# Token chunks of 512 and 784 instead of 656 and 640 in a two-pass hybrid encoder layer

## The chip, the core and the metric

The kernel runs on one core of a Trainium2 chip. The metric is the device time of one execution in microseconds (us); lower is better. Engines are named as the profile names them: PE (TensorE), PEld (its weight loads), DVE (VectorE), ACT (ScalarE), POOL (GpSimd) and SP (SyncE, which issues all DMAs here).

## What is computed

One encoder layer is applied to two requests: 1024 prompt tokens and 256 sample tokens, each preceded by the same 16 meta tokens; the width is 2048. The reference, cut down:

```python
u = rms_norm(h, norm_w) @ w_in                     # 2048 -> 6656 = 52 strips of 128
qa, ka, va, za, qb, kb, vb, zb = split(u)          # 8, 2, 2, 8, 8, 8, 8, 8 strips
qa, ka = rope(rms_norm(qa)), rope(rms_norm(ka));  qb, kb = rms_norm(qb), rms_norm(kb)
ya = global_gqa(qa, ka, va) * silu(za)             # 8 heads, 2 KV groups, all tokens
yb = neighbourhood_attention(qb, kb, vb, rpb) * silu(zb)   # 8 heads, window 8 x 16 + meta
return h + concat(ya, yb) @ w_out
```

## The kernel before

**Precision.** Every fp32 operand is split into a high part (rounded to fp32r) and a low part (the rest), and each product is three matmuls: high x high, high x low, low x high (`strips`, lines 131 to 133). Splitting a tile is a cast on ACT (line 50) and a subtraction on DVE (line 51).

**Two chunks.** All 16 + 256 + 1024 tokens don't fit on chip with the working buffers, so the input projection goes over the weights twice. Chunk 1 has the 16 meta tokens, the 256 sample tokens and the first 384 prompt tokens (T1 = 656); chunk 2 has the other 640 prompt tokens (T2). In a chunk the normalised x stays resident as 16 tiles (`kt`) of 128 rows, high and low. For each of the 52 strips, `strips` goes through 16 `kt`, and for each `kt` through the token blocks of the chunk. A block is one PSUM tile of at most 512 columns, so a chunk has two blocks: 272 + 384 (k and v strips) or 256 + 384 (q and z strips) in chunk 1, and 384 + 256 in chunk 2. That is 52 x 16 x 4 x 3 = 9984 matmuls.

**Weights.** In chunk 1 a strip's weights come in four DMAs (line 114), are split (lines 50 and 51), and the low part is also stored to DRAM (line 124). In chunk 2 the low part is read back (line 118) and only the cast on ACT is done again (line 119).

**x tiles.** `get_x` (lines 73 to 103) loads one `kt` into a ring of four tiles named `xr` (line 77; one of the four is held by the running sum `xacc`), ACT makes the high part (line 81), DVE the low part (82), ACT squares the ring tile in place (86) and DVE adds it to `xacc` (87), after which the ring tile is free. It is called from `strips` at the moment the first strip of a chunk needs that `kt`. The rings, the attention work buffers and all other pools are opened once in `build` (from line 957) and live through both chunks.

**Attention.** Chunk 1 runs the sample's 16 heads as their strips are done; the last two strips (v and z of the last head) are projected together, and then that head's attention runs. Its work tiles are `Sm`, `zs` (pool `mx`) and the six `t` tiles; the last of them is read by `put_y` (lines 229 to 239). In the second half of chunk 1 sums of `w_out` blocks are also made (`w_sums`: per projection either four loads or four stores of 256 KB). Chunk 2 first projects k and v of the first KV group together, then runs the prompt's 8 global heads (three strips and four query blocks for each), and then 24 remaining strips of the local heads between 28 blocks of local attention. v is turned into rows by PE transposes (line 173). `outproj` follows with its own pools; its matmuls (lines 827 to 829) have 320 columns.

The instructions are put in order by a scheduler at build time; every engine and the SP queue then run their lists in that order.

Of the kernel before, what the change touches and what calls it, by code (L numbers as in the profile page):

```python
# [27 lines left out]
C1P = 384  # L28
# [12 lines left out]
QA, KA, VA, ZA, QB_, KB, VB, ZB = 0, 8, 10, 12, 20, 28, 36, 44  # L41


class Kern:
# [27 lines left out]
    def get_x(self, kt):  # L72
        nc = self.nc
        if kt not in self.xs:
# [3 lines left out]
            h = self.x.tile([P, T], F32R, tag="xh", name="xh")  # L78
            l = self.x.tile([P, T], F32R, tag="xl", name="xl")
            w = self.nw[:, kt:kt + 1]  # L80
            nc.scalar.activation(h[:], r[:], AF.Copy, scale=w)  # L81
            nc.vector.scalar_tensor_tensor(out=l[:], in0=r[:], scalar=w, in1=h[:].bitcast(F32), op0=ALU.mult, op1=ALU.subtract)  # L82
# [5 lines left out]
            self.xs[kt] = (h[:], l[:])  # L88
            if kt == KT - 1:
                with self.tc.issue_after(self.lastx):  # L90
                    for d, c in self.consts:
                        nc.sync.dma_start(d[:], c)
# [4 lines left out]
                for o in range(0, T, 328):  # L97
                    n = min(328, T - o)
                    rr = self.rsqrt(self.eb[:, o:o + n], n)
                    nc.scalar.mul(self.rb[:, o:o + n], rr[:], -1.0)  # L100
# [3 lines left out]
    def strips(self, jobs, getx):  # L104
# [297 lines left out]

    def copy_km(self, k):
# [11 lines left out]
    def meta_tiles(self):  # L415

        self.npm = 0
        self.pms = [self.sm.tile([P, QB], F32R, tag=f"Pm{i}", bufs=1, name="Pm") for i in range(2)]
        self.vm3 = self.v.tile([P, P], F32R, tag="vm", name="vm3")
# [39 lines left out]
    def chunk1(self):  # L459
# [3 lines left out]
        ct = self.tab.tile([P, T1], F32, tag="bt", name="ropec")  # L463
        st = self.tab.tile([P, T1], F32, tag="st", name="ropes")
        B0, B1, BQ = (0, NMETA + NS), (NMETA + NS, C1P), (NMETA, NS)

        def k_strip(s, g, wc, rope):
            kt_ = self.k.tile([P, 2, T1], F32R, tag="k1", name="kc1")

            def evac(ps):  # L470
                for p, (o, n) in zip(ps, [B0, B1]):
                    rp = (ct[:, o:o + n], st[:, o:o + n]) if rope else None
                    self.qk_evac(p, o, n, wc, rp, [(0, n, kt_[:, 0, o:o + n], kt_[:, 1, o:o + n])])
                nc.sync.dma_start(self.kd[g][:, :, :NMETA], kt_[:, :, :NMETA].bitcast(F32))
                nc.sync.dma_start(self.kd[g][:, :, NMETA:], kt_[:, :, NMETA + NS:].bitcast(F32))
                return kt_, self.copy_km(kt_)
            return s, [B0, B1], evac

        def v_strip(s, g):
# [3 lines left out]
            vp = self.v.tile([P, 3 if loc else 6, P], F32 if loc else F32R, tag="v1", name="vp")  # L483

            def evac(ps):
                vt = self.v_rows(ps[0], *B0)
                tp = self.v_turn(vt, [0], NMETA)
                self.split(vm[:, 0:1, :], vm[:, 1:2, :], tp)
# [4 lines left out]
                vt = self.v_rows(ps[1], *B1)  # L493
                tp = self.v_turn(vt, [0, P, 2 * P])
                if loc:
                    nc.scalar.copy(vp[:], tp)
                    nc.sync.dma_start(self.vn[g - 2][:C1P].rearrange("(t p) d -> p t d", p=P), vp[:])
                else:
                    self.split(vp[:, :3, :], vp[:, 3:, :], tp)
                    nc.sync.dma_start(self.vd[g][:], vp[:].bitcast(F32))  # L500
# [3 lines left out]
            return s, [B0, B1], evac  # L504

        def q_strip(s, h, wc, rope):
            q = self.s.tile([P, 2, QB], F32R, tag="S", name="qs")

            def evac(ps):
                qp = [self.ev.tile([P, C1P], F32R, tag="ev", name="qp") for _ in range(2)]  # L510
                for p, (o, n), d in zip(ps, [BQ, B1], [(q[:, 0, :], q[:, 1, :]), (qp[0][:], qp[1][:])]):
                    rp = (ct[:, o:o + n], st[:, o:o + n]) if rope else None
                    self.qk_evac(p, o, n, wc, rp, [(0, n, *d)])
# [3 lines left out]
            return s, [BQ, B1], evac  # L517

        def z_strip(s, h):
            z = self.mx.tile([P, QB], F32, tag="mx", name="zs")  # L520

            def evac(ps):
                zp = self.ev.tile([P, C1P], F32, tag="ev", name="zp")
                self.z_evac(ps[0], *BQ, [(0, NS, z[:])])
                self.z_evac(ps[1], *B1, [(0, C1P, zp[:])])
                nc.sync.dma_start(self.zd[h][:, :C1P], zp[:])
                return z
            return s, [BQ, B1], evac
# [38 lines left out]
    def chunk2(self):  # L567
# [3 lines left out]
        ct = self.tab.tile([P, T2], F32, tag="bt", name="ropec2")  # L571
        st = self.tab.tile([P, T2], F32, tag="st", name="ropes2")
        self.consts = [(ct, io["ropec"][:, T1:]), (st, io["ropes"][:, T1:])]
        BL = [(0, 384), (384, 256)]
# [18 lines left out]
        def v_strip(s, g):  # L593

            v = [self.v.tile([P, 8, P], F32R, tag=f"v{i}", name="va") for i in range(2)]
            vm = self.load_vm(g)
            for i in range(2):
                nc.sync.dma_start(v[i][:, :3, :].bitcast(F32), self.vd[g][:, 3 * i:3 * i + 3, :])

            def evac(ps):  # L600
                for p, (o, n) in zip(ps, BL):
                    j, e = 3 + o // P, 3 + (o + n) // P
                    self.split(v[0][:, j:e, :], v[1][:, j:e, :], self.v_turn(self.v_rows(p, o, n), range(0, n, P)))
                return [(v[0][:, j, :], v[1][:, j, :]) for j in range(8)], vm
            return s, BL, evac

        def v_local(s, h):

            def evac(ps):
                for p, (o, n) in zip(ps, BL):  # L610
                    j, e = 3 + o // P, 3 + (o + n) // P
                    vt = self.ev.tile([P, n // P, P], F32, tag="ev", name="vl")
                    nc.scalar.copy(vt[:], self.v_turn(self.v_rows(p, o, n), range(0, n, P)))
                    nc.sync.dma_start(self.vn[h][P * j:P * e].rearrange("(t p) d -> p t d", p=P), vt[:])
            return s, BL, evac

        def v_windows(h):

            v = []
            for i in range(2):  # L620
                t = self.v.tile([P, 8, P], F32, tag=f"v{i}", name="vw")
                for j in range(2):
                    o = 32 * WIN0[2 * i + j]
                    nc.sync.dma_start(t[:, 4 * j:4 * j + 4, :], self.vn[h][:].rearrange("(t p) d -> p t d", t=4)[o:o + P])
# [92 lines left out]
        for h in range(NH):  # L717
            late += [qk_late(KB + h, kwb, self.k2d[2 + h]), qk_late(QB_ + h, qwb, self.q2d[8 + h]),
                     z_late(ZB + h, self.zd[8 + h]), v_local(VB + h, h)]
# [5 lines left out]
        for g in range(2):  # L725
            if g == 0:
                k, v = pr(k_strip(KA, 0, kw, True), v_strip(VA, 0))
            else:
                k, = pr(k_strip(KA + g, g, kw, True))
                v, = pr(v_strip(VA + g, g))  # L730
# [28 lines left out]
    def y_load(self, p, k):  # L759
# [6 lines left out]
        return [half(*x) for x in {1: [(k, 0)], 2: [(8 + k, 0)], 4: [(8 + k, 1)], 7: [(k, 0), (k, 1)],  # L766
                                   5: [(k, 1), (8 + k, 1)], 6: [(k, 0)], 3: [(8 + k, 0)]}[p]]

    def y_operand(self, p, k, r):
        nc = self.nc  # L770
        if p in (1, 2, 4):
            v = r[0]
        elif p == 7:
# [98 lines left out]
    def outproj(self, end_attention):  # L872
# [22 lines left out]
        for n in range(N):  # L895
# [19 lines left out]
            if n > 6:  # L915
# [14 lines left out]
    def build(self):  # L930
# [3 lines left out]
        with tc.tile_pool(name="dr", bufs=1, space=DRAM) as dp, tc.tile_pool(name="const", bufs=1) as cp, \  # L934
                tc.tile_pool(name="raw", bufs=4) as self.raw, tc.tile_pool(name="w", bufs=4) as self.w:
            self.kd = [dp.tile([P, 2, NMETA + C1P], F32, name=f"kd{g}") for g in range(10)]
            self.vd = [dp.tile([P, 6, P], F32, name=f"vd{g}") for g in range(2)]
            self.vn = [dp.tile([NP, P], F32, name=f"vn{h}") for h in range(NH)]
# [14 lines left out]
            with ExitStack() as ps, ExitStack() as es_y:  # L953
# [5 lines left out]
                es_pp, es_x, es_attn, es_xr, es_proj, es_late = (ExitStack() for _ in range(6))  # L959
                pool(es_pp, "pp", 4, space=PSUM)  # L960
                pool(es_x, "x", 16, side="right")
# [99 lines left out]
```

## Time and profile before

| | |
|---|---|
| median of 3 runs | 2250.45 us (2248.92 to 2253.45) |
| the profiled execution, its own time | 2249.38 us |
| its span, first to last instruction | 2247.6 us |
| PE busy | 2218.2 us, 99% of the span |
| DVE, ACT, POOL busy | 71%, 51%, 23% |

Matmuls overlap in the profile (each row reaches over the start of the next), so the time that one takes on PE is read from start to start, and not from the mean duration of a group. A granted clock of 1.00 is 2.4 GHz.

### The profile page before, as it was taken

To read this page: it belongs to the slowest core of one execution; us is meant where nothing else is said; L and a number is where in the kernel's file an instruction comes from. 1 tells how busy PE (TensorE), PEld (TensorE's weight loads), DVE (VectorE), ACT (ScalarE), POOL (GpSimd) and SP (SyncE) were. 2 spreads that over 40 slices of the span, in tenths; PEclk is the share of its full clock that TensorE was granted. 3 is DMA by queue.
4 is the path that set the end of the run, shared out by engine and by line. 5 is a ranking of instruction groups with operands and counts; after the bars stand their busy time and mean duration, and the time that the engine had idled before them with its cause. 6 is when DMAs were issued, how large, how long until landed. Compare 5 with 4: busy or idle time off the path is not lost.

```text
span 2247.6 us, 42246 instructions
## 1 busy us (share of the span) xinstructions
PE 2218.2 (99%) x15550; PEld 2208.7 (98%) x15550; DVE 1596.4 (71%) x2988; ACT 1141.5 (51%) x2432; POOL 526.5 (23%) x275
## 2 busy tenths in 40 slices
PE   7999999999999999999999999999999999999999
PEld 6999999999999999999999999999999999999999
DVE  5876677656666566999979998887665677636743
ACT  5554554443444466777667776655444454232220
POOL 0322222222222203332323332343333222000000
PEclk9999999999999999999999999999999999999999
DMA  7656578777777775444454344476767664845663
GB/s 238 196 185 185 176 225 254 246 238 246 243 243 235 228 241 152 126 122 123 140 149 126 112 134 138 151 219 207 221 201 215 211 194 127 276 152 162 198 210 112
DMA packets 279856, 424.54 MB, mean 189 GB/s; under 512 B 48576, under 2 KB 121184, under 8 KB 279648
## 3 DMA queue, kind: packets, MB, share of 16 engines
q1 hardware_dynamic: 279648, 421.84, 61.1%
q8 instruction: 122, 2.00, 0.4%
q14 instruction: 86, 0.70, 0.1%
HBM read 296.25 MB, written 118.90 MB: 185 GB/s over the span
## 4 chain that ended last, share of the span: by engine, by line
PE 90%; DVE 4%; DMA 3%; ACT 1%; POOL 1%; issue 1%; SPq 0%; DVEq 0%; POOLq 0%; ACTq 0%
PE pp L132 20%; PE pp L133 20%; PE pp L131 20%; PE pq L827 6%; PE pq L829 6%; PE pq L828 6%; DMA xr<-in_x 2%; PE po L392 1%; PE po L295 1%; PE po L293 1%; PE po L294 1%; PE sp L253 1%; PE sp L254 1%; PE sp L255 1%; DVE S L273 1%
## 5 line engine op out<-in xcount | busy, mean ns | idle before, releaser
L131 PE MATMUL pp<-xh,wh 128*128 128x384 f32 (+2 forms) x3328 | 1026.9, 312 | 16.9 <-ACT xh L81 16.9
L133 PE MATMUL pp<-xh,wl 128*128 128x384 f32 (+2 forms) x3328 | 1035.2, 312 | 0.0
L132 PE MATMUL pp<-xl,wh 128*128 128x384 f32 (+2 forms) x3328 | 1034.1, 311 | 0.4 <-DVE xl L82 0.2
L131 PEld LDWEIGHTS pp<-xh,wh 128*128 128x128 f32 x3328 | 625.7, 189 | 19.5 <-ACT xh L81 19.2
L132 PEld LDWEIGHTS pp<-xl,wh 128*128 128x128 f32 x3328 | 628.0, 189 | 1.8 <-DVE xl L82 1.8
L133 PEld LDWEIGHTS pp<-xh,wl 128*128 128x128 f32 x3328 | 628.1, 189 | 0.7
L51 DVE TENSOR_TENSOR wl<-wr,wh 128x512 fp32r<-128x512 f32 x320 | 236.4, 751 | 177.5 <-ACT wh L50 164.2
L141 POOL PARTITION_ALL_REDUCE m<-ms x104 | 237.0, 2279 | 399.6 <-ACT ms L139 264.0
L50 ACT CAST wh<-wr 128x512 fp32r<-128x512 f32 x320 | 193.7, 618 | 225.2 <-PE pp L132 150.9
L827 PE MATMUL pq<-ym,wh 128*128 128x320 f32 x896 | 276.5, 309 | 1.3 <-DVE vt L166 1.3
L828 PE MATMUL pq<-ym,wh 128*128 128x320 f32 x896 | 277.0, 309 | 0.0
L829 PE MATMUL pq<-ym,wl 128*128 128x320 f32 x896 | 276.9, 309 | 0.0
L222 POOL PARTITION_ALL_REDUCE tot<-a x80 | 168.4, 2105 | 439.7 <-DVE a L220 432.8
L205 POOL PARTITION_ALL_REDUCE ma<-m x80 | 114.2, 1427 | 460.3 <-DVE m L203 460.1
L827 PEld LDWEIGHTS pq<-ym,wh 128*128 128x128 f32 x896 | 168.2, 188 | 1.5 <-ACT ym L50 1.5
L829 PEld LDWEIGHTS pq<-ym,wl 128*128 128x128 f32 x896 | 168.3, 188 | 0.0
L828 PEld LDWEIGHTS pq<-ym,wh 128*128 128x128 f32 x896 | 168.3, 188 | 0.0
L119 ACT CAST wh<-wr 128x512 fp32r<-128x512 f32 x208 | 127.8, 615 | 56.5 <-PE pp L132 54.9
L57 ACT ACTIVATE rs_l<-m 128x384 f32<-128x384 f32 (+2 forms) x104 | 49.1, 472 | 121.4 <-DVE m L142 119.1
L257 ACT COPY S<-sp 128x512 f32<-128x512 f32 x136 | 78.6, 581 | 51.6 <-PE sp L255 45.0
L51 DVE TENSOR_TENSOR pl<-S,ph 128x512 fp32r<-128x512 f32 x136 | 98.7, 733 | 7.5 <-ACT ph L50 7.1
L61 DVE TENSOR_TENSOR rs_l<-m,rs_l 128x384 f32<-128x384 f32 (+2 forms) x104 | 75.4, 725 | 33.6 <-ACT rs_l L60 33.5
(200 smaller groups left out, 3396.9 us busy)
## 6 DMA issues: line engine op xcount, KB each, us to landing
wr<-in_w_in SPq DMA_DIRECT2D x416, 256.0 KB, 3.8
wld<-wl SPq DMA_DIRECT2D x208, 256.0 KB, 4.3
wl<-wld SPq DMA_DIRECT2D x208, 256.0 KB, 3.3
yr<-yd SPq DMA_DIRECT2D x72, 320.0 KB, 4.2
wq<-in_w_out SPq DMA_DIRECT2D x64, 256.0 KB, 5.5
td<-wq SPq DMA_DIRECT2D x64, 256.0 KB, 4.6
wr<-td SPq DMA_DIRECT2D x64, 256.0 KB, 3.6
wr<-in_w_out SPq DMA_DIRECT2D x48, 256.0 KB, 4.2
```

The costliest lines, as they stand in the source:

```text
L50: nc.scalar.copy(hi, full)
L51: return nc.vector.tensor_tensor(out=lo, in0=full, in1=hi.bitcast(F32), op=ALU.subtract).ins
L119: nc.scalar.copy(wh[:], w[:])
L131: nc.tensor.matmul(p[:, :n], wh[:, k, :], xh[:, o:o + n], start=first, stop=False)
L132: nc.tensor.matmul(p[:, :n], wh[:, k, :], xl[:, o:o + n], start=False, stop=False)
L133: nc.tensor.matmul(p[:, :n], wl[:, k, :], xh[:, o:o + n], start=False, stop=last)
L141: nc.gpsimd.partition_all_reduce(m2[:], ms[:], P, RED.add)
L205: nc.gpsimd.partition_all_reduce(ma[:], m1[:], P, RED.max)
L222: nc.gpsimd.partition_all_reduce(tot[:], a1[:], P, RED.add)
L827: nc.tensor.matmul(ps[:, b, :B], wh, yh[:, o], start=k == 0, stop=False)
L828: nc.tensor.matmul(ps[:, b, :B], wh, yl[:, o], start=False, stop=False)
L829: nc.tensor.matmul(ps[:, b, :B], wl, yh[:, o], start=False, stop=k == 7)
```

## The change

The first chunk gets 240 prompt tokens (T1 = 512), the second 784. Chunk 1 then has one block of 512 columns (k, v) or 496 (q, z), and chunk 2 two blocks of 392, for each product. 16 strips (q, k, v and z of local heads 4 to 7) neither store nor reload their low weight parts: chunk 2 splits them again. Chunk 1's pools are closed at its end, and chunk 2 opens its own in the same memory; a tile of a pool opened with `reuse_waits: "tile"` waits only for the old tiles that it lies over. Chunk 2 makes all of its 16 x tiles before its first strip, and the `xr` ring is then closed and the attention work pools are opened in its place. The v rows of all strips go through DRAM. Ring depths: `raw` 5 in chunk 1 and 3 afterwards (4 before), `ev` 8 in chunk 2 (9), `y` 1 in chunk 2 (2). In the output projection some operands are loaded straight into their final tile and split there.

```diff
-C1P = 384
+C1P = 240
+AGAIN = {a + h for a in (QB_, KB, VB, ZB) for h in range(4, 8)}
...
-                    if self.second:
+                    if self.second and s not in AGAIN:
...
-                if not self.second:
+                if not self.second and s not in AGAIN:
...
+    def rows_out(self, vt, n, dst, o):
...
+                nc.tensor.transpose(tp[:m, i, :], vt[:, x:x + m], self.ident[:])
...
+            nc.scalar.copy(t[:, :f, :], tp[:, :f, :])
+            nc.sync.dma_start(dst[o + a:o + a + P * f].rearrange("(t p) d -> p t d", p=P), t[:, :f, :])
...
-        B0, B1, BQ = (0, NMETA + NS), (NMETA + NS, C1P), (NMETA, NS)
+        B0, BQ = (0, T1), (NMETA, NS + C1P)
...
+        for kt in range(KT):
+            self.get_x(kt)
+        open_attention()
+        BL = [(0, T2 // 2), (T2 // 2, T2 // 2)]
...
+        def v_tiles(g):
...
+            nc.sync.dma_start(l[:].bitcast(F32), self.vn[g][:].rearrange("(t p) d -> p t d", p=P))
...
+        if p in (1, 2, 4):
+            t = self.ym.tile([P, 2, TH], F32R, tag="ym", name="ym")
+            self.nc.sync.dma_start(t[:, 1, :].bitcast(F32), self.yd[k if p == 1 else 8 + k][:, TH * (p == 4):][:, :TH])
+            return t
...
+                work = (("s", 5), ("ph", 2), ("sm", 2), ("mx", 2), ("t", 6))
...
+                with ExitStack() as es_1:
+                    pool(es_1, "x", 16, side="right")
+                    for name, bufs in (("raw", 5), ("tab", 1), ("k", 1), ("v", 1), *work, ("y", 2), ("one", 1), ("ev", 9), ("xr", 4)):
+                        pool(es_1, name, bufs)
+                    self.chunk1()
...
+                pool(es_x, "x", 16, side="right", **kw)
+                for name, bufs in (("one", 1), ("ev", 8)):
+                    pool(es_proj, name, bufs, side="right", **kw)
+                for name in ("k", "v", "tab", "q", "z"):
+                    pool(es_attn, name, 1, **kw)
+                pool(es_xr, "xr", 4, **kw)
...
+                def open_attention():
+                    es_xr.close()
+                    for name, bufs in (*work, ("y", 1)):
+                        pool(es_attn, name, bufs, **kw)
```

## Rows read from the trace of the kernel before

**Rows 1.** The page, busy time of each engine over the span.
```profile
PE 2218.2 (99%) x15550; PEld 2208.7 (98%) x15550; DVE 1596.4 (71%) x2988; ACT 1141.5 (51%) x2432; POOL 526.5 (23%) x275
```
**Rows 2.** The page, shares of the chain that ended last, by engine.
```profile
PE 90%; DVE 4%; DMA 3%; ACT 1%; POOL 1%; issue 1%; SPq 0%; DVEq 0%; POOLq 0%; ACTq 0%
```
**Rows 3.** Windows: stretch, length, busy us (instructions) per engine, PEclk, DMA share, GB/s.
```profile
0.00:50.00 50.00, 35.40 (x186) 32.20 (x187) 30.46 (x39) 29.36 (x42) 1.31 (x9) 0.97 0.73 222
...
805.00:840.00 35.00, 31.43 (x208) 30.56 (x208) 26.44 (x45) 26.29 (x49) 3.87 (x2) 0.95 0.80 257
1450.00:1900.00 450.00, 445.52 (x3182) 443.69 (x3182) 319.18 (x709) 228.99 (x519) 146.51 (x86) 1.00 0.65 200
...
1950.00:2000.00 50.00, 50.00 (x343) 50.00 (x342) 25.18 (x36) 16.49 (x29) 0.00 (x0) 1.00 0.62 200
```
**Rows 4.** PE groups by shape: count, busy us, mean ns of one, idle before.
```profile
L133 PE MATMUL pp<-xh,wl 128*128 128x384 f32 x1664 | 564.6, 339 | 0.0
...
L133 PE MATMUL pp<-xh,wl 128*128 128x256 f32 x1344 | 379.2, 282 | 0.0
...
L829 PE MATMUL pq<-ym,wl 128*128 128x320 f32 x896 | 276.9, 309 | 0.0
```
**Rows 5.** PE timeline around 1101 us: start, duration, instruction.
```profile
1100.67 0.34 PE L131 MATMUL pp<-xh,wh 128*128 128x384 f32 x1
...
1101.20 0.28 PE L131 MATMUL pp<-xh,wh 128*128 128x256 f32 x1
...
1102.27 0.34 PE L131 MATMUL pp<-xh,wh 128*128 128x384 f32 x1
...
1102.79 0.28 PE L131 MATMUL pp<-xh,wh 128*128 128x256 f32 x1
```
**Rows 6.** Waits of PE, whole span: total us, times, longest.
```profile
PE pp L131 <- ACT xh L81: 16.9, 8, 7.9
```
**Rows 7.** ACT timeline, the first and the last x tile of chunk 1.
```profile
7.01 0.84 ACT L81 ACTIVATE xh<-xr,nw 128x656 fp32r<-128x656 f32 x1 [0.26 <-DMA xr<-in_x]
...
46.77 0.84 ACT L81 ACTIVATE xh<-xr,nw 128x656 fp32r<-128x656 f32 x1 [0.60 <-DMA xr<-in_x]
```
**Rows 8.** SP timeline, two x loads of chunk 2, seven others between them.
```profile
807.19 0.33 SPq L77 DMA_DIRECT2D xr<-in_x  x1
...
831.76 0.33 SPq L77 DMA_DIRECT2D xr<-in_x  x1
```
**Rows 9.** Line 82: durations ns min/median/max; then the landing of line 77's DMAs.
```profile
L82 DVE SCALAR_TENSOR_TENSOR xl<-xr,nw,xh x32: 865/890/904, 7.9 to 838.5; 128x656 fp32r<-128x656 f32 x16, 128x640 fp32r<-128x640 f32 x16
...
DMA to landing us min/median/max: 2.8/4.5/6.7
```
**Rows 10.** PE timeline, first matmul after chunk 1's last strips.
```profile
804.99 0.19 PE L307 MATMUL sp<-qs,kc 128*128 128x64 f32 x1
```
**Rows 11.** DVE timeline, the last head of chunk 1: last readers of Sm and of tot.
```profile
823.13 1.21 DVE L215 TENSOR_TENSOR Pm<-Sm,Pm 16x256 fp32r<-16x256 f32 x1
...
830.58 0.41 DVE L232 SCALAR_TENSOR_TENSOR r<-tot,r 128x256 f32<-128x256 f32 x1
```
**Rows 12.** The chain, output matmuls of two sample heads in turn.
```profile
396.42 0.84 PE po L332 x8
457.00 0.84 PE po L332 x8
```
**Rows 13.** Windows of chunk 1, columns as in rows 3.
```profile
365.00:370.00 5.00, 5.00 (x37) 5.00 (x36) 4.20 (x8) 1.46 (x3) 0.00 (x0) 1.00 1.00 353
...
665.00:670.00 5.00, 5.00 (x36) 5.00 (x35) 2.69 (x6) 2.71 (x6) 0.00 (x0) 1.00 0.99 297
...
300.00:550.00 250.00, 250.00 (x1719) 249.65 (x1718) 169.18 (x305) 110.57 (x242) 58.44 (x28) 1.00 0.79 244
```
**Rows 14.** Groups by shape: the transposes, the low parts of the weights.
```profile
L173 PE MATMUL tp<-ident,vt 128*128 128x128 f32 x116 | 19.2, 272 | 0.0
...
L51 DVE TENSOR_TENSOR wl<-wr,wh 128x512 fp32r<-128x512 f32 x320 | 236.4, 751 | 177.5 <-ACT wh L50 164.2 <-DMA wr<-in_w_in 6.3 <-DMA wld<-wl 3.4
```

More of the change, by code (lines that the diff above doesn't have):

```diff
@@ L96, in get_x @@
                 nc.vector.tensor_scalar(out=self.eb[:], in0=self.eb[:], scalar1=EPS, scalar2=None, op0=ALU.add)
-                for o in range(0, T, 328):
-                    n = min(328, T - o)
+                for o in range(0, T, 392):
+                    n = min(392, T - o)
                     rr = self.rsqrt(self.eb[:, o:o + n], n)
@@ L401, in bias_table @@
         return tab
+    def rows_out(self, vt, n, dst, o):
+        nc = self.nc
+        for a in range(0, n, 4 * P):
+            offs = range(a, min(n, a + 4 * P), P)
+            full = [x for x in offs if x + P <= n]
+            t = self.ev.tile([P, 3, P], F32, tag="ev", name="vl")
+            tp = self.tp.tile([P, 4, P], F32, tag="tp", name="tp")
+            for i, x in enumerate(offs):
+                m = min(P, n - x)
+                nc.tensor.transpose(tp[:m, i, :], vt[:, x:x + m], self.ident[:])
+            f = len(full)
+            nc.scalar.copy(t[:, :f, :], tp[:, :f, :])
+            nc.sync.dma_start(dst[o + a:o + a + P * f].rearrange("(t p) d -> p t d", p=P), t[:, :f, :])
+            if f < len(offs):
+                m = n - offs[f]
+                t = self.ev.tile([m, P], F32, tag="ev", name="vl")
+                nc.scalar.copy(t[:], tp[:m, f, :])
+                nc.sync.dma_start(dst[o + n - m:o + n], t[:])
     def copy_km(self, k):
@@ L417, in meta_tiles @@
         self.npm = 0
-        self.pms = [self.sm.tile([P, QB], F32R, tag=f"Pm{i}", bufs=1, name="Pm") for i in range(2)]
-        self.vm3 = self.v.tile([P, P], F32R, tag="vm", name="vm3")
+        self.pms = [self.mt.tile([P, QB], F32R, tag=f"Pm{i}", name="Pm") for i in range(2)]
+        self.vm3 = self.mt.tile([P, P], F32R, tag="vm", name="vm3")
         for t in (*self.pms, self.vm3):
@@ L482, in v_strip @@
             vm = self.v.tile([NMETA, 2, P], F32R, tag="vm1", name="vm")
-            vp = self.v.tile([P, 3 if loc else 6, P], F32 if loc else F32R, tag="v1", name="vp")
             def evac(ps):
                 vt = self.v_rows(ps[0], *B0)
-                tp = self.v_turn(vt, [0], NMETA)
-                self.split(vm[:, 0:1, :], vm[:, 1:2, :], tp)
+                self.split(vm[:, 0:1, :], vm[:, 1:2, :], self.v_turn(vt, [0], NMETA))
                 if loc:
@@ L492, in evac @@
                     self.split(vs[:, :2, :], vs[:, 2:, :], self.v_turn(vt, [NMETA, NMETA + P]))
[L493 to L500, printed above, removed]
+                self.rows_out(vt[:, PS:], C1P, self.vn[g], 0)
                 for i, j in enumerate((0, 1, 0)):
@@ L516, in evac @@
                 return q
[L517 removed]
+            return s, [BQ], evac
         def z_strip(s, h):
@@ L771, in y_operand @@
         if p in (1, 2, 4):
-            v = r[0]
-        elif p == 7:
+            self.split(r[:, 0, :], r[:, 1, :], r[:, 1, :].bitcast(F32))
+            return r
+        if p == 7:
             v = r[0]
@@ L934, in build @@
         with tc.tile_pool(name="dr", bufs=1, space=DRAM) as dp, tc.tile_pool(name="const", bufs=1) as cp, \
[L935 removed]
+                tc.tile_pool(name="raw", bufs=3) as self.raw, tc.tile_pool(name="w", bufs=4) as self.w:
             self.kd = [dp.tile([P, 2, NMETA + C1P], F32, name=f"kd{g}") for g in range(10)]
[L937 to L938 removed]
+            self.vn = [dp.tile([NP, P], F32, name=f"vn{g}") for g in range(10)]
             self.vmd = [dp.tile([M3, P], F32, name=f"vmd{g}") for g in range(10)]
```

99 lines of the change are left out of this document (40 added, 59 removed).

## The prediction

> **What bounds the kernel now.** I read the page first: PE is busy 99% of the span and the next engine, DVE, 71% [rows 1], and the chain that ended last is 90% PE [rows 2]. So only two things can move the time: what PE's own work costs, and the few places where PE waits. The windows show where these are [rows 3]: 14.6 us without PE in the first 50 us, 3.6 us between 805 and 840 us, 4.5 us in all of 1450 to 1900 us. The list of PE's waits names the cause of the largest: 16.9 us for the high part of an x tile [rows 6]. At 805 to 840 us the granted clock is 0.95 of 2.4 GHz as well, so 5% of 35 us is 1.8 us of lost PE work there, 5.3 us in all.
>
> **Term 1, matmuls.** The columns stay the same (1296 for k and v, 1280 for q and z); the blocks per product go from four to three, so 52 x 16 x 3 = 2496 of 9984 matmuls go. What one of them costs beyond its columns is read in two ways. Start to start, six 384-column matmuls take 0.53 + 0.52 us and nine 256-column ones 1.07 us [rows 5]: 175.0 and 118.9 ns, a slope of 0.438 ns per column, which leaves 6.7 ns at no columns. The 320-column ones take 50 us / 343 = 145.8 ns [rows 3]; with the slope of the mean durations, (339 - 282) / 128 = 0.445 [rows 4], 3.3 ns is left. I take the middle, 5 ns: 2496 x 5 = **-12 us**. Bounds: with the slope of the upper pair, (339 - 309) / 64 = 0.469, the fixed part is 145.8 - 150 = below zero, so 0; with one column per cycle at 2.4 GHz it is 145.8 - 133.3 = 12.5 ns, so -31 us. My value lies near the lower end because both long baselines do.
>
> The Trainium skill ("TensorE: Matmul & The Clock Gate", section "Wait — 56ns, not 53.3ns?") gives a warm matmul N / 2.4 GHz plus about 2.5 ns whatever N is. This trace does not agree: 320 columns take 12.5 ns more than N / 2.4. By the page's fixed part the term would be an estimated 2496 x 2.5 ns = -6 us, and the sum below 6 us higher.
>
> **Term 2, the way from chunk 1 to chunk 2.** Before, the x ring outlives chunk 1, so x tiles of chunk 2 are loaded while the last strips run. After, the ring lies where chunk 1's work tiles were. From the pool list: chunk 1 puts raw (10,240 bytes per partition), tab (4608), k (4480), v (3072), s (10,240), ph (8192), sm (2048), mx (4096) and t (6144) one after another; chunk 2 puts k (8704), v (8192), tab (6272), q (8192) and z (4096), so its ring begins at 35,456 and has four tiles of 3136. The first two lie over ph and the first Sm, both long free; the third over the second Sm and mx, the fourth over the last head's `zs` and a `t` tile. Of the four, one is `xacc`. With two early places, at least one of the first three users (first x tile, `xacc`, second x tile) gets a late one; I assume both of the latter do. So the first x tile can come early, and the next, and the sum that frees the first, wait for the last head's attention.
>
> Let E be the end of chunk 1's last strips (804.99 us in this trace [rows 10]). That head's Sm was last read from 823.13 us on, its tot at 830.58 [rows 11]: 18 and 26 us after E, shared with the x tiles' own ACT and DVE work. With those held back I estimate 10 and 14 us; bounds 5 and 26. A ring tile's round is load, high part, low part, square, sum, each after the other. In the first chunk 16 tiles of 656 columns went from 7.01 to 46.77 us [rows 7], 2.65 us each; times 784/656 is 3.2. In the second, nine loads from 807.19 to 831.76 us [rows 8] are 3.07 us apart at 640 columns, beside attention; times 784/640 is 3.8. I take 3.1: of the round only the transfer and the four passes grow, the landing (2.8 to 6.7 us [rows 9]) has a part that does not. The fourth tile's load then starts at E + 15, lands and is cast by E + 20, and the last of the 16 is ready at 20 + 12 x 3.1 = E + 57; its matmuls end at E + 59. PE's own work up to there is 16 x 12 matmuls of 392 columns (0.179 us: 5 ns and 0.445 per column), 34.4 us, and some 3 us of attention: 22 us without work, 5.3 us of which were there before. Of these 17 I take off 2 for one more tile that comes early (2.1 us of matmuls): **+15 us**, bounds -5 (no wait at all) and +25. Behind the waiting load on SP stand the last head's stores, which nothing needs soon, and weight loads, for which three tiles are in hand; behind the first tile's square on ACT stand only casts of tiles that are late anyway. The 16 x loads move ahead of the first strips' weight loads, which the priority in `strips` pulls forward as before: nothing.
>
> **Term 3, the start.** The same ring with 512 columns: 16 x 2.65 x 512/656 instead of 16 x 2.65 us is 9 us earlier, while PE's work in them shrinks by 6.6 us: 96 pairs of matmuls (16 tiles, two strips, three products) of 0.126 + 0.175 us become 96 of 0.233. PE idles 2.7 us less: **-2 us**, bounds -6 and +2.
>
> **Term 4, DMA in chunk 1.** A sample head with local attention takes 457.00 - 396.42 = 60.6 us [rows 12], and at 244 GB/s [rows 13] that is 14.8 MB. Its four strips shrink from 57.1 to 43.9 us (48 matmuls per block and strip, by term 1's line), so a head takes 47.4 us; 48 transfers of 0.262 MB (weights, low parts, `w_out` sums) stay and the other 2.2 MB shrink to some 1.5: 14.1 MB, 297 GB/s for heads 0 to 3, and 209 for heads 4 to 7, whose 4.2 MB of low parts are not stored. Five-us stretches in which the 16 engines were busy throughout moved 297 to 353 GB/s [rows 13]. So four heads run near the edge of it: **+2 us**; bounds 0 (353 GB/s suffices) and +12 (280 GB/s through 190 us).
>
> **Small terms.** Transposes: two leftover rows of 8 per v strip in chunk 2, 20 more at up to 0.11 us, +1. The 64 splits made again cost DVE 0.75 us each [rows 14], 48 us late in the 450 us where DVE is busy 71% [rows 3], beside strips whose PE time grows by a fifth: nothing, as long as PE leads; without that cover 3 us a strip. Their 128 DMAs less, and a longer strip per attention block: -1 of the 4.5 us lost there, bounds -4 and +5. v through DRAM: the store and load (some 8 us on SP) come two strips before v is needed, 34 us; behind the waiting load on SP stand weight loads with three tiles in hand: nothing, at most +2. Output projection: the first operand's load must now wait for the last x tiles instead of only its split; +1, bounds 0 and +4. `y` with one tile, `ev` 8, `raw` 3: stores and loads of 3 to 4 us against 5 us and more between uses: nothing, at most +3.
>
> **Sum.** -12 + 15 - 2 + 2 + 1 - 1 + 1 = +4 us on the profiled execution's 2249.4, which is 1.1 us under the median: **2255 us** against 2250.45, 0.2% slower. About 0.2% (4.5 us) is what a measurement of this kernel can tell from no change, so the forecast stands on that edge.
>
> **Rivals.**
> R1, *a slow ring*: x tiles at 3.8 us each, as rows 8 scaled say, because weights of two strips (0.26 MB per tile) load beside 0.40 MB of x. The last tile is ready at 20 + 12 x 3.8 = E + 66 and term 2 is 9 us larger: 2264 us. It decides once a round is over 3.5 us. For it: the rows 8 rate was measured at this very place; against: attention shared ACT and DVE then.
> R2, *no new stall*: term 2 is about zero, since the scheduler places the last head's attention early or the ring tiles come free as the strips run. Then the matmuls decide: 2255 - 15 = 2240 us, faster. For it: only two of four ring tiles lie under late work; against: they are taken early, and PE had nothing else to do while waiting for x even before [rows 6].
> R3, *fewer matmuls save little*: the time goes with the columns, the fixed part is between nothing and half of what I take, and the change doesn't save what it counts: 2255 + 6 to 2255 + 12, 2261 to 2267 us. For it: the slope of the upper pair of rows 4; against: the two long baselines of term 1. The page named there states a fixed part of this size; by it the time would be an estimated 2261 us.
>
> **How the numbers follow.** The forecast has 0.45, with a range of its own of 2248 to 2262; R2 0.28 (2234 to 2246); R1 0.15 (2259 to 2271); R3 0.12 (2259 to 2268). Faster by over 0.2% (below 2246): R2 and 0.01 of the forecast, 0.29. Within: 0.24 of the forecast. Slower (over 2255): 0.20 of it, R1 and R3, 0.47. The range 2237 to 2266 leaves out about 0.08 on either side.
>
> **What would show it.** In the changed profile: 7488 projection matmuls, with 512 columns some 233 ns and 392 some 179 ns from start to start (term 1); chunk 1 ending near 635 us; after it 15 to 25 us without PE, put down to the high part of x, with PE's first long gap ending when the second x tile lands (term 2); an idle time of 12 to 13 us in the first 45 us (term 3); 290 GB/s or more and no PE idle in the sample's local heads 0 to 3 (term 4). The forecast is wrong if PE is idle under 8 us between the chunks (R2), or over 28 us there (R1), or if start-to-start times are on a line through zero (R3).

## The result, and the profile after

The changed kernel takes 2257.7 us against 2250.7 us for the kernel before on the same chip: ratio 1.0031, 95% interval 1.0021 to 1.0041, some 7 us slower. Two of the ten executions of the changed kernel took 5624 and 7064 us at a granted clock of 1.00, for a reason that is not known, and the ratio and its interval are of the other eight. The profiled execution's span is 2256.6 us, 9.0 us more than before.

The page, busy times and the chain's shares by engine ([rows 1, 2] before):

```profile
PE 2210.6 (98%) x13074; PEld 2095.9 (93%) x13074; DVE 1625.9 (72%) x2862; ACT 1131.3 (50%) x2276; POOL 517.8 (23%) x249
...
PE 89%; DMA 4%; DVE 4%; ACT 1%; issue 1%; POOL 0%; SPq 0%; DVEq 0%; POOLq 0%; ACTq 0%
```

The 2476 fewer matmuls (2496 of the projections less, 20 transposes more) are there, and PE still leads. Now its groups by shape (count, busy us, mean ns, idle before) and its timeline, for what one matmul takes from start to start ([rows 4, 5]):

```profile
L133 PE MATMUL pp<-x,wh 128*128 128x392 f32 x1664 | 570.0, 343 | 0.1
...
L133 PE MATMUL pp<-x,wh 128*128 128x512 f32 x320 | 128.2, 401 | 0.2
```

```profile
500.05 0.40 PE L132 MATMUL pp<-x,wh 128*128 128x512 f32 x1
...
501.91 0.40 PE L134 MATMUL pp<-x,wl 128*128 128x512 f32 x1
...
720.04 0.34 PE L133 MATMUL pp<-x,wh 128*128 128x392 f32 x1
...
722.19 0.34 PE L133 MATMUL pp<-x,wh 128*128 128x392 f32 x1
```

Eight steps of 512 columns take 1.86 us, 232.5 ns each; twelve of 392 take 2.15 us, 179 ns each. The prediction said 233 and 179. The windows (columns as in [rows 3]):

```profile
0.00:50.00 50.00, 33.00 (x117) 23.13 (x118) 27.58 (x41) 27.10 (x45) 1.32 (x9) 1.00 0.77 248
600.00:650.00 50.00, 43.67 (x205) 36.07 (x203) 25.36 (x48) 23.03 (x48) 12.17 (x5) 0.91 0.37 110
650.00:700.00 50.00, 38.50 (x182) 36.95 (x182) 27.59 (x30) 27.21 (x34) 0.00 (x0) 0.82 0.65 199
300.00:350.00 50.00, 48.97 (x233) 40.70 (x232) 36.13 (x65) 23.97 (x48) 11.92 (x5) 1.00 0.94 317
350.00:400.00 50.00, 50.00 (x238) 41.60 (x237) 33.27 (x56) 22.25 (x45) 9.92 (x4) 1.00 0.92 307
...
1450.00:1900.00 450.00, 448.84 (x2796) 447.51 (x2795) 326.10 (x654) 210.10 (x452) 136.57 (x74) 1.00 0.44 141
```

In the first 50 us PE has no work for 17.0 us, 14.6 before. Between 600 and 700 us it has none for 17.8 us, and the granted clock falls to 0.91 and 0.82. The local stage (1450 to 1900) idles 1.2 us instead of 4.5, and at 307 to 317 GB/s PE idles 1 us of 100 (300 to 400 us). PE's waits, total, times and longest ([rows 6]):

```profile
PE pp L132 <- ACT x L82: 28.2, 9, 8.3
PE po L330 <- DVE Pm L216: 4.6, 1, 4.6
PE sp L254 <- ACT qs L51: 2.2, 2, 1.1
```

The wait for x's high part has grown from 16.9 to 28.2 us. Where it sits is seen in the timeline after chunk 1's last strips, whose last matmul starts at 637.9 us (E below; 804.8 us in the trace before):

```profile
646.96 1.20 DVE L216 TENSOR_TENSOR Pm<-Sm,Pm 16x256 fp32r<-16x256 f32 x1
...
650.43 0.42 DVE L239 TENSOR_TENSOR y<-po,zs 128x256 f32<-128x256 f32 x1 [0.43 <-PE po L333]
...
651.67 0.40 SPq L241 DMA_DIRECT2D yd<-y  x1
652.11 1.44 SPq L78 DMA_DIRECT2D xr<-in_x  x3
...
655.94 0.95 ACT L82 ACTIVATE x<-xr,nw 128x784 fp32r<-128x784 f32 x1 [6.47 <-DMA xr<-in_x]
...
656.94 1.68 PE L132 MATMUL pp<-x,wh 128*128 128x392 f32 x4 [6.56 <-ACT x L82]
658.42 0.53 PE L133 MATMUL pp<-x,wh 128*128 128x392 f32 x1
658.75 0.53 PE L134 MATMUL pp<-x,wl 128*128 128x392 f32 x1
```

All 16 x loads of chunk 2 stand on SP behind the last head's y store (651.67); the first goes out 14 us after E. In the trace before, seven of the 16 were out by E, the first 53 us ahead of it. So the last head's attention runs alone, PE waits 6.56 us for the first cast, and its matmuls then start at half clock (658.42 to 658.75 is 0.33 us for 392 columns):

```profile
640.00:645.00 5.00, 1.88 (x7) 0.99 (x6) 2.68 (x9) 2.45 (x8) 1.06 (x1) 0.61 0.59 170
645.00:650.00 5.00, 1.79 (x9) 1.79 (x9) 3.69 (x7) 2.96 (x7) 2.25 (x1) 0.50 0.12 34
650.00:657.00 7.00, 0.44 (x3) 0.26 (x2) 1.26 (x4) 1.06 (x2) 0.00 (x0) 0.50 0.75 225
657.00:662.00 5.00, 5.00 (x16) 5.00 (x17) 3.53 (x4) 3.40 (x4) 0.00 (x0) 0.54 0.44 135
662.00:670.00 8.00, 8.00 (x46) 8.00 (x46) 4.85 (x6) 5.67 (x7) 0.00 (x0) 1.00 0.60 170
```

**Where the 9 us come from.** To set stages side by side I sum, over the matmuls that start in a stretch, the time to the next start less that shape's usual time at full clock, within 1 ns of its median (118.1 ns for 256 columns, 125.3 for 272, 146.7 for 320, 175.3 for 384, 178.5 for 392, 223.8 for 496, 233.0 for 512; 112 for all shorter ones). That is what PE "loses" there, idle and slow clock together.

| stretch | before | after | difference |
|---|---|---|---|
| all matmuls at these usual times | 2200.0 | 2189.2 | -10.8 |
| lost, 0 to 150 us | 16.5 | 15.0 | -1.5 |
| lost, 150 to 350 us (global sample heads) | 0.0 | 7.5 | +7.5 |
| lost, 85 us from E - 10 | 5.8 | 26.2 | +20.4 |
| lost, 1450 to 1840 us | 10.2 | 2.6 | -7.6 |
| lost, from 1840 us (output projection) | 0.8 | 2.5 | +1.7 |
| lost, the rest | 1.0 | -0.2 | -1.2 |

The projections alone are worth -13.1 us by these times; the 20 transposes more, counted at 112 ns, take 2.2 back. The sum is +8.5 us; the first matmul starts 0.4 later.

Each column is one execution, and such losses scatter. Two runs below (the 196-column cuts of 3, and 4) do the same as the changed kernel, in the same order on every engine, up to 440 us, and still lose 18.7 and 15.7 us by 150 us and 11.2 and 10.2 from 150 to 350 us. So the rows around E and of the global sample heads are clear of the scatter, and the -1.5 of the first 150 us is not. The border at 1840 us cuts the stages a little apart: the first output matmul starts at 1835.1 us before and at 1843.6 after. With that as the border, the local stage goes from 10.2 to 3.6 us and the output projection from 0.9 to 1.5.

### The profile page after: what moved, and what is told of

The parts are those of the page before. It is cut to its first block, busy times and chain, and to the rows that moved or that the text cites. A ratio compares the mean times of both kernels' runs of the same rounds, so it can differ in the third digit from the quotient of the medians.

```text
span 2256.6 us, 36723 instructions
## 1 busy us (share of the span) xinstructions
PE 2210.6 (98%) x13074; PEld 2095.9 (93%) x13074; DVE 1625.9 (72%) x2862; ACT 1131.3 (50%) x2276; POOL 517.8 (23%) x249
## 4 chain that ended last, share of the span: by engine, by line
PE 89%; DMA 4%; DVE 4%; ACT 1%; issue 1%; POOL 0%; SPq 0%; DVEq 0%; POOLq 0%; ACTq 0%
PE pp L132 19%; PE pp L133 19%; PE pp L134 19%; PE pq L838 6%; PE pq L839 6%; PE pq L837 6%; DMA xr<-in_x 2%; PE po L393 2%; PE sp L254 1%; PE sp L256 1%; PE sp L255 1%; PE po L295 1%; PE po L296 1%; PE po L294 1%; DMA wr<-in_w_in 1%
## 5 line engine op out<-in xcount | busy, mean ns | idle before, releaser
L132 PE MATMUL pp<-x,wh 128*128 128x392 f32 (+2 forms) x2496 | 889.7, 361 | 28.2 <-ACT x L82 28.2
L133 PE MATMUL pp<-x,wh 128*128 128x392 f32 (+2 forms) x2496 | 896.7, 359 | 0.3
L134 PE MATMUL pp<-x,wl 128*128 128x392 f32 (+2 forms) x2496 | 894.2, 358 | 0.1
L132 PEld LDWEIGHTS pp<-x,wh 128*128 128x128 f32 x2496 | 470.7, 189 | 63.1 <-ACT x L82 31.8
L133 PEld LDWEIGHTS pp<-x,wh 128*128 128x128 f32 x2496 | 471.5, 189 | 34.6 <-DVE x L83 2.9
L134 PEld LDWEIGHTS pp<-x,wl 128*128 128x128 f32 x2496 | 471.5, 189 | 32.2 <-DVE wl L52 0.7
L52 DVE TENSOR_TENSOR wl<-wr,wh 128x512 fp32r<-128x512 f32 x384 | 273.7, 724 | 134.0 <-ACT wh L51 107.5
L142 POOL PARTITION_ALL_REDUCE m<-ms x78 | 223.8, 2869 | 350.6 <-ACT ms L140 301.1
L223 POOL PARTITION_ALL_REDUCE tot<-a x80 | 187.3, 2341 | 475.8 <-DVE a L221 457.4
L206 POOL PARTITION_ALL_REDUCE ma<-m x80 | 98.9, 1236 | 452.8 <-DVE m L204 446.1
L274 DVE TENSOR_TENSOR S<-S,ma 128x512 f32<-128x512 f32 x136 | 103.9, 820 | 8.0 <-POOL ma L206 7.8
L275 ACT ACTIVATE S<-S 128x512 f32<-128x512 f32 x136 | 83.5, 628 | 38.4 <-DVE S L274 38.2
```

Source lines behind the costliest of these rows:

```text
L52: return nc.vector.tensor_tensor(out=lo, in0=full, in1=hi.bitcast(F32), op=ALU.subtract).ins
L132: nc.tensor.matmul(p[:, :n], wh[:, k, :], xh[:, o:o + n], start=first, stop=False)
L133: nc.tensor.matmul(p[:, :n], wh[:, k, :], xl[:, o:o + n], start=False, stop=False)
L134: nc.tensor.matmul(p[:, :n], wl[:, k, :], xh[:, o:o + n], start=False, stop=last)
L142: nc.gpsimd.partition_all_reduce(m2[:], ms[:], P, RED.add)
L206: nc.gpsimd.partition_all_reduce(ma[:], m1[:], P, RED.max)
```

## The experiments

Theory A: the matmuls are worth what was predicted, and the way from chunk 1 to chunk 2 costs more than that, because chunk 2's x ring lies over tiles that chunk 1's last head still uses. Its rivals: the ring's own pace (P), a time that goes with the columns alone (C), DMA in chunk 1 (D).

**1. The ring over free memory.** In the changed kernel only the order of chunk 1's pool list is altered:

```diff
-... ("v", 1), *work, ("y", 2), ("one", 1), ("ev", 9), ("xr", 4)):
+... ("v", 1), work[0], ("xr", 4), *work[1:], ("y", 2), ("one", 1), ("ev", 9)):
```

> Edit: chunk 1's xr pool moves in the list from behind ev to between s and ph, so that chunk 2's x ring lies over chunk 1's xr and ph, which the last head does not use; everything else as in the changed kernel (2257.7 us). Theory A (the ring is late because it lies over tiles of the last head, so its loads stand on SP behind that head's last store, and PE loses some 20 us between the chunks): the first x load of chunk 2 is issued before chunk 1's last strips end, what PE loses between 600 and 700 us falls from 26 us to between 6 and 12, and the time is 2239 to 2246 us, under the kernel before. Rival P (the pace of the ring, 2.5 us per tile of 784 columns against 2.15 us of matmuls, with the casts beside attention, sets the loss wherever the ring lies): PE still loses 20 us or more there, 2252 to 2258 us.

2245.1 us, ratio to before 0.9985 (0.9976 to 0.9994): 12.6 us under the changed kernel (10.9 by each one's distance from the kernel before) and faster than the kernel before. Its SP timeline, its x casts after 590 us (count, ns min/median/max, first to last start) and two windows:

```profile
596.80 0.37 SPq L78 DMA_DIRECT2D xr<-in_x  x1
...
639.77 0.33 SPq L78 DMA_DIRECT2D xr<-in_x  x1
...
663.26 0.46 SPq L241 DMA_DIRECT2D yd<-y  x1
```

```profile
L82 ACT ACTIVATE x<-xr,nw x16: 936/949/955, 637.7 to 684.5; 128x784 fp32r<-128x784 f32 x16
```

```profile
600.00:650.00 50.00, 49.44 (x243) 42.20 (x242) 29.34 (x47) 26.80 (x49) 9.32 (x4) 1.00 0.52 158
650.00:700.00 50.00, 43.97 (x237) 42.47 (x236) 30.91 (x39) 31.85 (x51) 9.29 (x3) 0.97 0.69 215
```

Three loads go out from 40 us before E on, the y store now stands behind eleven of the sixteen, and the first cast comes at E + 0.7 instead of E + 18. PE loses 9.9 us around E instead of 26.2. Nothing else was edited (some pools of chunk 1 move by 8192 bytes), so the place of the ring is what costs it. P falls: this ring is slower (15 steps in 46.8 us, 3.12 us each, against 2.54 from 655.94 to 694.0 in the changed kernel, where no attention runs beside it) and the kernel is faster.

**2. The pools alone, on the kernel before.** Blocks, chunks and weights as in the kernel before, but pools of their own for each chunk, and chunk 2's 16 x tiles made ahead of its first strip (not shown below):

```diff
-                pool(es_x, "x", 16, side="right")
...
-                pool(es_xr, "xr", 4)
+                with ExitStack() as es_1:
+                    pool(es_1, "x", 16, side="right")
+                    for name, bufs in (("tab", 1), ("k", 1), ("v", 1), *work, ("y", 2), ("one", 1), ("ev", 9), ("xr", 4)):
+                        pool(es_1, name, bufs)
+                    self.chunk1()
+                pool(es_x, "x", 16, side="right", **kw)
...
+                pool(es_ring, "xr", 4, **kw)
...
+                self.chunk2(open_attention)
```

> Edit: the kernel before (384 tokens of the prompt in chunk 1, blocks of 272 and 384, no strip made twice) with pools of their own for each chunk: chunk 1's are closed, chunk 2's x ring then lies over chunk 1's Sm, zs and t tiles. Theory A: the loss between the chunks comes with the pools alone; the x loads of chunk 2 stand behind the last head's y store, PE loses 18 to 26 us in the 100 us around the end of chunk 1 instead of 6, and the time is 2262 to 2271 us against 2250.5. Rival P (the larger tiles of 784 columns cause it): PE loses 5 to 9 us there and the time is 2248 to 2254 us.

2272.8 us, ratio 1.0105 (1.0091 to 1.0118): 23.7 us more than the kernel before, just over A's interval. SP's timeline, the x casts of chunk 2, and the 85 us after 795 us, first of this run and then of the kernel before:

```profile
816.96 0.33 SPq L240 DMA_DIRECT2D yd<-y  x1
817.34 14.47 SPq L77 DMA_DIRECT2D xr<-in_x  x7
```

```profile
L81 ACT ACTIVATE xh<-xr,nw x16: 812/828/832, 822.4 to 869.5; 128x640 fp32r<-128x640 f32 x16
```

```profile
795.00:880.00 85.00, 62.01 (x367) 59.98 (x366) 35.48 (x56) 39.43 (x70) 7.13 (x3) 0.82 0.58 181
```

```profile
795.00:880.00 85.00, 81.43 (x552) 80.56 (x551) 52.82 (x92) 54.38 (x108) 16.55 (x7) 0.98 0.69 218
```

E is 803.4 here, so the first load is at E + 14, the first cast at E + 19, and PE loses 32.4 us instead of 5.8: the same stall, without the 784 columns. With the one edit of run 1 on top (chunk 1's `xr` between `s` and `ph`):

> Edit: the run with the kernel before and pools of their own for each chunk (2272.8 us), with chunk 1's xr pool moved between s and ph, so that chunk 2's ring lies over chunk 1's xr and ph. Theory A (not the closing of the pools costs the 22 to 24 us, but the place of the ring over tiles that the last head still uses): 2247 to 2255 us, at the kernel before or just above it, and PE loses 5 to 9 us around the end of chunk 1. Rival W (closing chunk 1's pools makes chunk 2 wait for something else as well, the x tiles or the ev and one pools on the other side): 2260 us or more.

2253.8 us, ratio 1.0015 (1.0006 to 1.0024), and in the same window

```profile
795.00:880.00 85.00, 79.29 (x516) 75.83 (x515) 52.21 (x87) 54.41 (x106) 14.27 (x6) 0.98 0.68 213
```

PE loses 10.9 us, a little over the 5 to 9 expected. So W falls: the rest of the edit (pools closed, x tiles made ahead) costs some 3 us, the place of the ring the other 20. This run and run 1 differ in the change's other parts (blocks, chunks, strips split again) with the ring free in both: 3.0 us over and 3.9 us under the kernel before, so those parts are worth some -7 us.

**3. What a matmul costs beyond its columns.** First, the count of before restored in chunk 2, in place of the three matmuls of each block (the block that is cut starts at column 392: it is the second of the two, where the expectation says the first; the count is the same):

```diff
+cuts = ((0, 196), (196, 196)) if o == 392 else ((0, n),)
+for w, x, f, e in ((wh, xh, first, False), (wh, xl, False, False), (wl, xh, False, last)):
+    for i, m in cuts:
+        nc.tensor.matmul(p[:, i:i + m], w[:, k, :], x[:, o + i:o + i + m], start=f and i == 0, stop=e and i + m == n)
```

> Edit: the first of the two 392-column matmuls of each product in chunk 2 is issued as two of 196 columns into the same PSUM tile: 2496 matmuls more, as many as the kernel before had, the same columns, tiles, transfers and order. Theory A (each matmul costs some 5 to 6 ns beyond its columns, 14 us for 2496): 2269 to 2275 us, with some 92 ns from start to start for 196 columns (0.445 per column and 5). Rival C (the time goes with the columns alone): 2257 to 2260 us and 87 ns. By the page's fixed part of 2.5 ns (the Trainium skill, TensorE: Matmul & The Clock Gate, section on 56 against 53.3 ns) an estimated 2264 us. If start to start is above 100 ns, something else than the fixed part (the weight load of each) bounds matmuls this short, and the run bounds the term from above only.

2376.7 us, ratio 1.0569 (1.0554 to 1.0583): 119 us more, outside every theory. PE's timeline:

```profile
900.10 0.59 PE L135 MATMUL pp<-x,wh 128*128 128x196 f32 x4
900.53 0.38 PE L135 MATMUL pp<-x,wl 128*128 128x196 f32 x2
900.75 0.54 PE L135 MATMUL pp<-x,wh 128*128 128x392 f32 x2
```

Four matmuls of 196 columns take 0.43 us and the next two 0.22: 108 and 110 ns each, not 92 (the median over the run is 111). Two of them in place of one of 178.5 ns cost some 43 ns, 2496 times: 108 us, most of the 119. (In this one trace chunk 1, where nothing was edited, is 6.6 us longer, too.) That is a floor under short matmuls and says little of the fixed part. So the cut was moved to chunk 1, with pieces of 240 columns or more (`cuts = ((0, 256), (256, n - 256)) if n > 392`):

> Edit: in chunk 1 each 512-column matmul is issued as 256 and 256 columns, each 496-column one as 256 and 240, into the same PSUM tile: 2496 matmuls more than the changed kernel, as many as before, no piece shorter than 240 columns; the 196-column pieces of the run before ran into a floor of some 111 ns. Theory A (the fixed part, from the start-to-start times of the traces: 2 x 118.1 - 233.0 = 3.2 ns for 960 of them, 118.1 + 111.4 - 223.8 = 5.7 ns for 1536): 12 us more than the changed kernel, 2267 to 2272 us. Rival C (columns alone): 2256 to 2261 us. Rival F (the floor of 111 ns and not a fixed part is all that a cut costs, and chunk 1's pieces of 240 columns lie just on it): 2258 to 2262 us.

2274.9 us, ratio 1.0113 (1.0097 to 1.0128), 17.2 us over the changed kernel. The cut lies in chunk 1 alone, so its price is read from when chunk 2's x loads begin; this run, then the changed kernel (count, ns, first to last start):

```profile
L78 SPq DMA_DIRECT2D xr<-in_x x16: 327/328/436, 664.4 to 709.6; - x16
```

```profile
L78 SPq DMA_DIRECT2D xr<-in_x x16: 327/328/438, 652.1 to 695.1; - x16
```

12.3 us later; E moves by 12.7 (637.9 to 650.6), 5.1 ns for each of the 2496. Since E scatters by some us (644.6 in the run before), the steps are a second reading: without the longest and the shortest tenth, the pieces take 119.7 ns (256 columns) and 110.2 (240) from start to start, where the whole matmuls took 233.1 (512) and 223.8 (496). That is 6.3 and 6.1 ns more per cut, some 15 us. C, which allows 3 us, falls; so does F, since 256 columns lie above the floor and cost as much. A cut costs 5 to 6 ns, as A has it, though the time lies 3 us above A's range. The Trainium skill ("TensorE: Matmul & The Clock Gate", section "Wait — 56ns, not 53.3ns?") has 2.5 ns, an estimated 6 us; this run, with 5 to 6 ns, does not agree. The span grew by 15.8 us; the other 3 lie after E, where the matmuls are the same, and what makes them was not found.

**4. All low parts kept** (`AGAIN = set()`).

> Edit: the set of strips whose low parts are made twice is empty: all 52 are stored in chunk 1 and loaded in chunk 2, 33.6 MB more to move than in the changed kernel. Theory A (transfers are hidden even at 300 to 317 GB/s in chunk 1, and the splits made again cost PE nothing): 2255 to 2261 us, 300 GB/s or more in heads 4 to 7 too, and no more PE idle there. Rival D (DMA is at its edge in chunk 1, and the set buys time): 2263 to 2275 us, with PE waiting for the weights' high or low part between 450 and 620 us.

2259.8 us, ratio 1.0049 (1.0035 to 1.0063); its interval overlaps the changed kernel's. A window of heads 4 to 7, which now store their low parts too:

```profile
450.00:500.00 50.00, 50.00 (x240) 41.76 (x238) 32.94 (x55) 22.09 (x44) 9.91 (x4) 1.00 0.91 300
```

PE is not idle there at 300 GB/s (nor anywhere from 450 to 600 us), so D falls. The span is 2.3 us longer, but 2.7 us more are lost between 150 and 350 us, ahead of every strip that differs: nothing shows that the set buys time.

**5. q ahead of z in the global sample heads** (the two `pr` lines of chunk 1's first loop swapped), for the 7.5 us between 150 and 350 us.

> Edit: the changed kernel (2257.7 us), with q's strip ahead of z's in the sample heads of chunk 1 that attend to all keys. Theory A (between 150 and 350 us PE loses 7.5 us beyond its matmuls, against nothing in the kernel before, because a head's two strips take 21.5 us instead of 28.2 and q's evacuation, on 496 columns at once, ends right where the scores need it; z is needed only at the end of the head): the waits of the scores for q (2.2 us) go, the loss between 150 and 350 us falls to 2 to 4 us, and the time is 2 to 6 us under the changed kernel's. Rival B (the loss there is the chain of the attention itself, which is as long whichever strip comes first): 2255 to 2260 us.

2259.4 us, ratio 1.0039 (1.0026 to 1.0051); PE still loses 7.4 us there. Its waits for q went from 2.2 to 1.2 us and others came in their place (0.9 for the high part of the probabilities, 0.7 for the low part, 0.7 for the q of a local head). So the swap does not mend it. That a head's attention has 21.5 us of strips to hide behind instead of 28.2 remains possible, and untested; it can hardly be all, since with the same strips only 4.0 to 4.7 us are lost there in the runs with eight ring tiles below that keep this order.

**6. A deeper ring.** Eight `xr` tiles in chunk 1 and six in chunk 2, on run 1:

> Edit: as the run with the ring over free memory (chunk 1's xr between s and ph), and eight xr tiles in chunk 1, six in chunk 2, all of these six over chunk 1's xr and ph. Theory A (with the place mended, what PE still loses between the chunks, 6.6 us without work between 600 and 700 us, and part of the 17 us of the first 50 us, waits for the round of a ring tile): the high part of x is waited for 8 to 14 us instead of 18.6, and the time is 2237 to 2243 us, 2 to 8 us under that run's 2245. Rival P (DMA and the casts set the pace, not the number of tiles): 2243 to 2247 us.

2232.1 us, ratio 0.9913 (0.9899 to 0.9927), 5 us under A's range; the wait for the high part of x is 11.2 us, inside it. The first 50 us (33.00 busy in the changed kernel) and the casts of chunk 2:

```profile
0.00:50.00 50.00, 40.34 (x160) 31.67 (x161) 35.11 (x54) 33.68 (x61) 8.58 (x11) 1.00 0.95 328
```

```profile
L82 ACT ACTIVATE x<-xr,nw x16: 933/950/955, 635.3 to 668.1; 128x784 fp32r<-128x784 f32 x16
```

The start gives some 10 us: at the same DMA engines the ring of four had left 23% of their time unused. But E is 624.5, and the first cast comes at E + 10.8 although five loads went out 36 to 40 us before E. Two runs take this apart: four tiles in chunk 2 again, and that with `ph` as the last pool of chunk 1's list.

> Edit: as the run with eight xr tiles in chunk 1 and six in chunk 2 (2232.1 us), but four in chunk 2 again. Theory A (the gain of that run came from chunk 1's start, where PE idles 9.7 us of the first 50 instead of 15.7, and not from chunk 2's ring): 2229 to 2235 us, the same 9 to 11 us lost after chunk 1's end. Rival B (the two more tiles in chunk 2 carried half of the gain): 2236 to 2242 us.

2240.0 us, ratio 0.9955 (0.9943 to 0.9968). A fails here: PE loses 18.1 us around E (625.9) instead of 10.2, so chunk 2's two more tiles were worth 8 us of that gain, as B said.

> Edit: as the run with eight and four xr tiles, with chunk 1's ph pool moved to the end of the list. With eight tiles chunk 1's list reaches 134,272 and its last pool, ev, lies under chunk 2's first x tile (128,992 to 135,264); ph, which the last head does not use, takes that place. Theory A (the first cast into an x tile waits for the last head's ev tiles, as the ring's loads did for its zs and t): the first cast comes at most 2 us after the end of chunk 1's last strips instead of 10, PE loses 3 to 8 us around it, and the time is 2 to 6 us under that of the run with eight and four: 2224 to 2232 us. Rival B (the casts stand behind the last head's attention on ACT, wherever the x tile lies): the first cast again some 10 us after, the same time within 2 us.

2231.2 us, ratio 0.9918 (0.9904 to 0.9932), 8.8 us under the run before it, more than the 2 to 6 expected, although PE still loses 10.0 us around E, over the 3 to 8 expected. Casts of chunk 2, with eight and four (E = 625.9) and with `ph` last (E = 625.4):

```profile
L82 ACT ACTIVATE x<-xr,nw x16: 932/947/956, 637.0 to 681.8; 128x784 fp32r<-128x784 f32 x16
```

```profile
L82 ACT ACTIVATE x<-xr,nw x16: 937/949/954, 626.1 to 672.9; 128x784 fp32r<-128x784 f32 x16
```

E + 11.1 became E + 0.7. With eight ring tiles, chunk 1's `ev` had come to lie under chunk 2's first x tile: the same fault as the ring's, one pool further. With q ahead of z on top:

> Edit: the run with ph moved to the end of chunk 1's list (2231.2 us), with q's strip ahead of z's as in the run before. Theory A: 2 to 4 us under that run, 2227 to 2230 us. Rival B: 2230 to 2233 us. Either way it should be the fastest of all runs here, or equal to the fastest.

2238.2 us, ratio 0.9945 (0.9933 to 0.9957): 7 us slower than without the swap, against both theories: PE loses 8.3 us between 150 and 350 us instead of 4.3, 2.7 of it in waits for the probabilities' high part, and 4 us more after 700 us, in chunk 2, where it waits 2.4 us for a q. Why the swap does this stays open.

**7. Both places mended, six tiles in chunk 2** (chunk 1's list, against that of run 6):

```diff
-... (("raw", 5), ("tab", 1), ("k", 1), ("v", 1), work[0], ("xr", 8), *work[1:], ("y", 2), ("one", 1), ("ev", 9)):
+... (("ev", 9), ("tab", 1), ("k", 1), ("v", 1), ("xr", 8), work[1], work[0], *work[2:], ("y", 2), ("one", 1), ("raw", 5)):
```

> Edit: eight xr tiles in chunk 1 and six in chunk 2, and chunk 1's list put in the order ev, tab, k, v, xr, ph, s, sm, mx, t, y, one, raw: the six ring tiles lie over xr and ph, and chunk 2's first x tile over weight tiles that are free before the last strips end. Theory A (the two places together: the first cast comes within 2 us of the end of chunk 1's last strips, as in the run with ph last, and the two more ring tiles are worth the 8 us that they were worth between the runs with six and with four): the loss in the 85 us around that end is 2 to 5 us, the time 2222 to 2228 us, the fastest of all runs here. Rival B (with the first x tile free in time, the ring of four already gives all there is): 2229 to 2233 us, as the run with ph last.

2225.9 us, ratio 0.9903 (0.9887 to 0.9920): the fastest version, 1.0% under the kernel before and some 30 us under the changed one. Its casts, the windows around E (625.4), and PE's largest wait:

```profile
L82 ACT ACTIVATE x<-xr,nw x16: 932/939/957, 626.1 to 661.0; 128x784 fp32r<-128x784 f32 x16
```

```profile
590.00:640.00 50.00, 49.62 (x247) 42.94 (x246) 31.90 (x48) 28.32 (x50) 8.64 (x4) 1.00 0.53 167
640.00:690.00 50.00, 48.67 (x277) 47.98 (x276) 34.46 (x49) 34.53 (x60) 13.61 (x4) 1.00 0.72 221
```

```profile
PE pp L132 <- ACT x L82: 11.2, 4, 8.4
```

Around E PE loses 2.7 us and the clock stays at 1.00. Of the 11.2 us that are left of the wait, 1.3 lie here and the rest in the first 50 us. Three versions in the stretch around E:

| kernel | first load | first cast | last cast | lost around E | time |
|---|---|---|---|---|---|
| changed | E + 14.2 | E + 18.0 | E + 56 | 26.2 | 2257.7 |
| ring over free memory | E - 40 | E + 0.7 | E + 48 | 9.9 | 2245.1 |
| all places free, 8 and 6 tiles | E - 40 | E + 0.7 | E + 36 | 2.7 | 2225.9 |

## Why the prediction was right

2255 us was forecast, with 2237 to 2266; 2257.7 was measured, on the side and by the mechanism that the forecast gave. Its +4 on the profiled execution was +9.

**Term 1** (-12): right. -13.1 us by the two traces, 12.7 to 15 us when the count alone is put back in chunk 1. R3 falls by that run.

**Term 2** (+15): the mechanism right, the size 5 us short: +20.4, inside its bounds. The step that failed is "so the first x tile can come early". By the pool list two of the four ring tiles were free, yet the build's scheduler put every x load behind the last head's y store, so the first was out at E + 14 and cast at E + 18, and PE's first long gap ended with it, not with the second tile. Why the scheduler did so when only some of the tiles were late is not shown; with all four free (run 1) it put three loads ahead of E. That the term was only 5 us short is due to errors that partly cancel: the tiles then came 2.54 us apart, not 3.1, with no attention beside them, so the last cast started at E + 56, where the sum had it done at E + 57; and stretches at half clock, which the term did not have, cost extra (2.4 us for the 16 matmuls up to 662 us alone). Where the loads come early the 3.1 holds (3.12 in runs 1 and `ph` last). The 2 us taken off for "one more tile that comes early" should have stayed. R1 falls: its pace of 3.8 us was never reached, and the faster kernel of run 1 has the slower ring. R2 falls for this kernel, but its 2240 us is close to what run 1 gives (2245.1) once the place is mended.

**Term 3** (-2): not confirmed. The -1.5 over the first 150 us is inside the scatter, and the sign that was to show it failed: PE has no work for 17.0 of the first 45 us, not 12 to 13. **Term 4** (+2): 0; 307 to 317 GB/s passed beside a busy PE, and so did 33.6 MB more. The local stage was put at -1 and gained 3.3 us by PE's idle time (6.6 by what PE loses up to the first output matmul); the output projection was put at +1 and costs 0.6 behind that border.

**Not in the sum:** 7.5 us in the global sample heads. The prediction looked at chunk 1's strips for DMA alone and not at what hides a head's attention when its strips shrink by a fourth; that this is the cause is not shown. The local stage's gain, larger than forecast, nearly cancels it, which is luck and not foresight.

## What to carry to other kernels

When pools are closed and opened again between two stages, write down which old tiles each new ring, and each tile that the ring feeds, lies over, and when those are last read; put the work tiles that end late under something that starts late. One wait for such a tile does not stay one wait: it stands in an in-order DMA queue and holds every prefetch behind it. Fewer, longer matmuls gave here what the start-to-start times said, so a change that pays for them with memory should be judged with that memory laid out well.

## What was not expected of the hardware

Short matmuls that each load their weights took some 111 ns from start to start, however few their columns: the median is 111 for 196 columns, 108 for the 128-column transposes, 111 to 112 for the 64-column matmuls of the attention and 111 for 240 columns, while 256 take 118. Only above that do the times here follow the line of 0.445 ns per column and 5 ns. Whether the weight load makes this floor is not shown. And a few idle gaps cost more than their length: with PE busy 4.1 of 17 us, the granted clock stood at 0.50 (1.2 of 2.4 GHz) when the x tiles came, and some 15 matmuls went at 0.33 us each before it was 1.00 again (from 662 us on).
